# The FFN norm's sums and transposes at fixed early places, and groups of 4, 9 and 9 FFN steps in place of 5, 9 and 8

## The chip, the cores and the metric

The kernel runs on one core of one Trainium2 chip. Its time is the device time of one execution in microseconds (us). Five engines run their own queues of instructions and wait for each other by semaphores: TensorE (PE; its weight loads are PEld), VectorE (DVE), ScalarE (ACT), GpSimd (POOL) and SyncE (SP), which here issues the loads from memory.

## The reference

Two layers of a decoder trunk on a sequence of 512 with a model width of 1024: three mixers side by side, then a gated MLP. What the change touches is the MLP of each layer, all in float32:

```python
h = rmsnorm(x, norm_ffn_g[l])
gu = jnp.einsum('bsd,df->bsf', h, w_ffn_in[l])
g_ff, u_ff = gu[..., :D_FF], gu[..., D_FF:]
g_ff = causal_dwconv(g_ff, ffn_conv_w[l], ffn_conv_b[l])
x = x + jnp.einsum('bsf,fd->bsd', jax.nn.silu(g_ff) * u_ff, w_ffn_out[l])
```

`rmsnorm` divides x by the root of the mean of its squares over the 1024 channels and multiplies by a gain. D_FF is 2816 = 22 x 128.

## The kernel before

**Tiles.** x lies transposed in eight tiles x[0] to x[7] of 128 channels by 512 positions. A float32 product is made of three matmuls (`mm3`, L159 to L161): each operand is split into a high part, rounded to float32r on ACT (`hi_...`, L150 or L166), and the rest, computed on DVE (`lo_...`, L151 or L167), and PE adds hi x hi, hi x lo and lo x hi into one PSUM tile. The names of loads, casts and splits follow the tile: raw_w2, hi_w2, lo_w2.

**The FFN** (`ffn`, once per layer) has 22 steps of 128 channels of D_FF, in groups. For each group the steps make their activations act0, act1, ..., and then `rows` adds the group's share of the down projection to x, one output tile d after the other: its PSUM tiles are called p2, the group, d (p203 is group 0, d = 3). Group 0's steps are `plain`, the others `seven`.

- `plain(f)`: pg is the gate projection (8 x 3 matmuls of 512 columns on xg, the split x), pu the upper one (as many). DVE multiplies pg by the norm (rB, into pad), convolves it (c, with ACT's share), ACT applies SiLU, DVE forms u = pu x rB x c, and ACT and DVE split it into act.
- `seven(f)` makes both projections with seven products of half size (Strassen-Winograd): 7 x 4 x 3 matmuls of 256 columns into the PSUM tiles pa and pb. It needs sums of weight blocks (s31, s24, on DVE, split to h31, l31, h24, l24) and X[0] to X[3], sums of the *normalised* x.
- `halves(k)` makes X[k]: two tiles of x times gain and rB (xn), four sums of them (xt), and their splits. The list `todo` holds k = 0 to 3; a call is made after some steps of group 0 and the last one in its rows.
- The norm (`norm_x`): squares of x[k] on ACT, added on DVE (ssf), summed over channels by four small matmuls (pssf), the inverse root on DVE (twelve tiny instructions on rf), four transposes on PE (prf), and a copy on ACT to rB. In the FFN it is called in plain step 0, between pg and pu.

**Buffers that set the order.** Weights are loaded into a ring of four raw tiles (tag raw). Their splits have three slots when a load is more than 512 wide and two (tag "b") when it is 512 or less. `rows` loads a row's weights in one load of width x 128 columns, or in two (512 and the rest) when the group has more than eight steps: 640 for five steps, 512 and 640 for nine, 1024 for eight. PSUM has four tiles for projections.

**What sets the order.** The code is recorded instruction by instruction; a scheduler then orders each engine's instructions by its own model of time, by priority (weight loads and splits, and the blocks of seven steps that make weight sums, have high priority) and by what is free. Each engine runs its list in that order. `tc.keep_in_program_order` holds an instruction at its recorded place.

Of the kernel before, what the change touches and what calls it, by code (L numbers as in the profile page):

```python
# [15 lines left out]
ALU = mybir.AluOpType  # L16
# [4 lines left out]
P = 128  # L21
# [6 lines left out]
DFF = 2816  # L28
FT = DFF // P

GROUPS = (5, 9, 8)
HALF = S // 2
BUCKETS = 32
MAX_DIST = 128
# [19 lines left out]
def trunk(ctx, tc, xT, wr, wh, wt, wda, wret, wsc, wo, wf, w2, par, lamp, relb, onehot, mask, rope, gtab, out):  # L54
# [14 lines left out]
    def temp(name, w=S):  # L69
        return tp.tile([P, w], F32, tag="s", name=name, bufs=6, padded_shape=[P, S])  # L70
# [62 lines left out]
    def load_w(src, name):  # L133
        n = int(np.prod(src.shape[1:]))
        with tc.high_priority():
            raw = wp.tile([P, n], F32, tag="raw", bufs=4, name="raw_" + name, padded_shape=[P, D])
            ordered(nc.sync.dma_start(raw if len(src.shape) == 2 else raw.rearrange("p (b n) -> p b n", b=src.shape[1]), src))
        return raw

    def split_w(raw, name):  # L140
        n = int(np.prod(raw.shape[1:]))
        with tc.high_priority():
            tag, bufs = ("", HL) if 2 * n > D else ("b", 2)
            hi, lo = [
                wp.tile([P, n], F32R, tag=t + tag, name=f"{t}_{name}", padded_shape=[P, D if n > D // 2 else D // 2], bufs=bufs)
                for t in ("hi", "lo")
            ]
            flat = len(raw.shape) == 2
            h, w = [t if flat else t.rearrange("p (b n) -> p b n", b=raw.shape[1]) for t in (hi, lo)]
            A.copy(h, raw)  # L150
            V.tensor_tensor(w, raw, h.bitcast(F32), ALU.subtract)  # L151
        return hi, lo
# [90 lines left out]
    def norm_x(name):  # L243

        ss = temp(f"ss{name}")
        A.activation(ss, x[0], AF.Square)
        for k in range(1, KT):
            sq = temp(f"sq{k}{name}")
            A.activation(sq, x[k], AF.Square)
            V.tensor_tensor(ss, ss, sq, ALU.add)  # L250
        ps = aux(f"pss{name}")
        for st in range(ST):
            T.matmul(ps[:, st : st + 1], ss[:, st * P : (st + 1) * P], ones[:, 0:1], start=True, stop=True)
        ms = small(4, f"ms{name}")
        V.tensor_scalar(ms, ps[:, 0:4], 1.0 / D, EPS, ALU.mult, ALU.add)
        r = sp.tile([P, 4], F32, tag="r", name=f"r{name}", bufs=2)
        rsqrt(r, ms, 4, name)
        pr = transposes(lambda st: r[:, st : st + 1].broadcast_to([P, P]), f"pr{name}")
        rB = sp.tile([P, S], F32, tag="rB", name=f"rB{name}", bufs=1)
        A.copy(rB, pr)  # L260
        return r, rB

    def project(xg, ps, w):

        for k, xk in enumerate(xg):
            sl = slice(k * P, (k + 1) * P)
            mm3(ps, (w[0][:, sl], w[1][:, sl]), xk, k == 0, k == len(xg) - 1)

# [9 lines left out]
    def transposes(src, name):  # L278

        ps = aux(name)  # L280
        for st in range(ST):
            T.transpose(ps[:, st * P : (st + 1) * P], src(st), ident)
        return ps

    def conv(dst, padt, wcol, bcol):
# [458 lines left out]
    def ffn(l, fp):  # L744
# [3 lines left out]
        pt = pars[l]  # L748
        L = f"L{l}"
        xg = [split_x(l, G_FFN, f"f{L}", k) for k in range(KT)]  # L750
        norm = []
        X = [fp.tile([P, 2, 7, HALF], F32R, name=f"X{k}{L}") for k in range(KT // 2)]

        def sums4(name):
# [20 lines left out]
        def plain(f):  # L775
            both = wf[l, f].rearrange("p (b n) -> p b n", n=S)
            ps = main(f"pg{f}{L}")
            project(xg, ps, split_w(load_w(both[:, 1::2], f"fg{L}{f}"), f"fg{L}{f}"))
            if not norm:
                norm.append(norm_x(f"f{L}")[1])  # L780
            padt = pads[f % 2]
            V.tensor_tensor(padt[:, 2 : S + 2], ps, norm[0], ALU.mult)
            c = temp(f"c{f}{L}")
            wc = FF_W + 3 * f
            conv(c, padt, lambda t: pt[:, wc + t : wc + t + 1], pt[:, FF_B + f : FF_B + f + 1])
            A.activation(c, c, AF.Silu)
            ps = main(f"pu{f}{L}")
            project(xg, ps, split_w(load_w(both[:, 0::2], f"fu{L}{f}"), f"fu{L}{f}"))
            u = temp(f"u{f}{L}")
            V.tensor_tensor(u, ps, norm[0], ALU.mult)  # L790
            V.tensor_tensor(u, u, c, ALU.mult)
            return split2(u, pairN(f"act{f}{L}"))

# [184 lines left out]
```

## Time and profile before

| | us |
|---|---|
| runs: median, lowest, highest of 3 | 1524.24, 1523.73, 1524.32 |
| the profiled execution, its span | 1523.98, 1522.2 |
| granted TensorE clock, mean | 1.000 |
| FFN of layer 0: plain steps start, rows of group 0 start, first seven step starts | 413.35, 469.18, 497.87 |
| FFN of layer 1: the same | 1167.46, 1223.28, 1251.96 |

All places are us from the span's start. In a row of the timeline stand start, duration, engine, line, operation, output<-inputs, and in brackets how long the engine had been idle and what ended that. Durations overlap a little at the ends, so costs in a row of equal work are better read from start to start.

### The profile page before, as it was taken

What the parts mean: (1) busy time and instruction counts of PE and PEld (TensorE: products, weight loads), DVE (VectorE), ACT (ScalarE), POOL (GpSimd) and SP (SyncE); (2) the same over time, 40 slices, a digit from 0 to 9 for tenths busy, and PEclk for the clock granted to TensorE, in tenths of its full rate; (3) what the DMA queues carried; (4) which work ended last, traced back from release to release, by engine and by line L of the source; (5) the groups of instructions that cost most, each with busy time, mean ns of one, the idle gap of its engine ahead of it and who ended that gap; (6) DMA issues with size and microseconds to landing.
All of it is one profiled execution on the core that took longest, in us unless ns stands there. A gap on an engine that the chain in (4) does not pass through costs nothing.

```text
span 1522.2 us, 22065 instructions
## 1 busy us (share of the span) xinstructions
PE 1513.5 (99%) x8510; PEld 1339.4 (88%) x8510; DVE 1103.4 (72%) x2074; ACT 733.5 (48%) x1304; POOL 13.0 (1%) x26
## 2 busy tenths in 40 slices
PE   9999999999999999999999999999999999999998
PEld 7899988888887999899789999888888889988996
DVE  8588787554669996796656887865545899957963
ACT  4555665333445564464425565643333556634641
POOL 1000000000000000000100000000000000000000
PEclk9999999999999999999999999999999999999999
DMA  6322222232323322522422222222322233234322
GB/s 212 115 73 81 87 84 90 76 104 83 108 71 108 116 93 72 169 84 84 132 76 93 74 91 87 83 84 83 110 85 89 80 109 111 88 93 139 112 60 80
DMA packets 51145, 147.24 MB, mean 97 GB/s; under 512 B 5623, under 2 KB 6022, under 8 KB 51040
## 3 DMA queue, kind: packets, MB, share of 16 engines
q1 hardware_dynamic: 50224, 143.38, 28.5%
q0 software_dynamic: 816, 2.46, 0.6%
q8 instruction: 67, 1.10, 0.3%
q14 instruction: 38, 0.31, 0.1%
HBM read 143.70 MB, written 2.11 MB: 96 GB/s over the span
## 4 chain that ended last, share of the span: by engine, by line
PE 96%; DVE 2%; DMA 1%; issue 0%; ACT 0%; SPq 0%; ACTq 0%; DVEq 0%
PE pnrvgL L161 1%; PE pnrvgL L159 1%; PE pnrvgL L160 1%; PE pnrqkL L160 1%; PE pnrqkL L161 1%; PE pnrqkL L159 1%; PE pnh2L L161 1%; PE pnh2L L159 1%; PE pnh3L L160 1%; PE pnh3L L161 1%; PE pnh1L L161 1%; PE pnh2L L160 1%; PE pnh3L L159 1%; PE pnh1L L160 1%; PE pnh0L L159 1%; PE pnh1L L159 1%
## 5 line engine op out<-in xcount | busy, mean ns | idle before, releaser
L150 ACT CAST hi_tL<-raw_tL 128x1024 fp32r<-128x1024 f32 x60 | 62.9, 1049 | 115.6 <-issue 14.7
L150 ACT CAST hi_w2L<-raw_w2L 128x640 fp32r<-128x640 f32 (+2 forms) x64 | 49.5, 782 | 86.8 <-PE p214L L160 10.4
L151 DVE TENSOR_TENSOR lo_tL<-raw_tL,hi_tL 128x1024 fp32r<-128x1024 f32 x60 | 73.4, 1223 | 15.9 <-ACT hi_tL L150 15.6
L151 DVE TENSOR_TENSOR lo_w2L<-raw_w2L,hi_w2L 128x640 fp32r<-128x640 f32 (+2 forms) x64 | 56.0, 886 | 28.7 <-ACT hi_w2L L150 28.7
L150 ACT CAST hi_fbL<-raw_f1L 128x1024 fp32r<-128x1024 f32 x34 | 35.7, 1050 | 38.8 <-PE pa8L L160 6.8
L151 DVE TENSOR_TENSOR lo_fbL<-raw_f1L,hi_fbL 128x1024 fp32r<-128x1024 f32 x34 | 41.4, 1219 | 5.1 <-ACT hi_fbL L150 5.0
L150 ACT CAST hi_oL<-raw_oL 128x1024 fp32r<-128x1024 f32 x16 | 16.9, 1054 | 58.1 <-issue 25.2
L150 ACT CAST hi_faL<-raw_f0L 128x512 fp32r<-128x512 f32 x34 | 21.1, 622 | 28.1 <-DMA raw_f0L<-in_wf 10.0
L151 DVE TENSOR_TENSOR lo_fuL<-raw_fuL,hi_fuL 128x1024 fp32r<-128x1024 f32 x10 | 12.2, 1223 | 19.6 <-ACT hi_fuL L150 19.6
L151 DVE TENSOR_TENSOR lo_faL<-raw_f0L,hi_faL 128x512 fp32r<-128x512 f32 x34 | 23.3, 684 | 3.7 <-ACT hi_faL L150 3.7
L150 ACT CAST hi_fuL<-raw_fuL 128x1024 fp32r<-128x1024 f32 x10 | 10.5, 1051 | 31.1 <-issue 17.5
L150 ACT CAST hi_nrvgL<-raw_nrvgL 128x1024 fp32r<-128x1024 f32 x8 | 8.4, 1050 | 29.7 <-PE pnrvgL L161 13.5
L150 ACT CAST hi_fgL<-raw_fgL 128x1024 fp32r<-128x1024 f32 x10 | 10.5, 1054 | 24.1 <-issue 16.0
L151 DVE TENSOR_TENSOR lo_oL<-raw_oL,hi_oL 128x1024 fp32r<-128x1024 f32 x16 | 19.6, 1224 | 2.8 <-ACT hi_oL L150 2.8
L151 DVE TENSOR_TENSOR lo_nrvgL<-raw_nrvgL,hi_nrvgL 128x1024 fp32r<-128x1024 f32 x8 | 9.8, 1221 | 12.5 <-ACT hi_nrvgL L150 12.5
L151 DVE TENSOR_TENSOR lo_nh0L<-raw_nh0L,hi_nh0L 128x768 fp32r<-128x768 f32 x8 | 7.6, 956 | 13.1 <-ACT hi_nh0L L150 13.1
L150 ACT CAST hi_bdL<-raw_bdL 128x512 fp32r<-128x512 f32 x16 | 9.9, 618 | 12.6 <-issue 4.2
L150 ACT CAST hi_nrqkL<-raw_nrqkL 128x1024 fp32r<-128x1024 f32 (+1 forms) x9 | 8.4, 947 | 13.9 <-issue 13.9
L150 ACT CAST hi_nh0L<-raw_nh0L 128x768 fp32r<-128x768 f32 x8 | 6.7, 838 | 15.2 <-PE pnh0L L161 7.8
L151 DVE TENSOR_TENSOR lo_fgL<-raw_fgL,hi_fgL 128x1024 fp32r<-128x1024 f32 x10 | 12.2, 1221 | 2.2 <-ACT hi_fgL L150 2.2
L151 DVE TENSOR_TENSOR lo_nrqkL<-raw_nrqkL,hi_nrqkL 128x1024 fp32r<-128x1024 f32 (+1 forms) x9 | 9.8, 1103 | 5.2 <-ACT hi_nrqkL L150 5.2
L150 ACT CAST hi_nh3L<-raw_nh3L 128x768 fp32r<-128x768 f32 x8 | 6.7, 838 | 11.5 <-PE ptg16L L160 5.3
(8471 smaller groups left out, 5967.6 us busy)
## 6 DMA issues: line engine op xcount, KB each, us to landing
raw_tL<-in_wt SPq DMA_DIRECT2D x60, 512.0 KB, 3.3
raw_f0L<-in_wf SPq DMA_DIRECT2D x34, 512.0 KB, 3.7
raw_f1L<-in_wf SPq DMA_DIRECT2D x34, 512.0 KB, 3.7
raw_w2L<-in_w SPq DMA_DIRECT2D x32, 320.0 KB, 2.9
raw_oL<-in_wo SPq DMA_DIRECT2D x16, 512.0 KB, 3.4
raw_w2L<-in_w SPq DMA_DIRECT2D x16, 512.0 KB, 3.5
raw_fgL<-in_wf SPq DMA_DIRECT2D x10, 512.0 KB, 4.0
raw_fuL<-in_wf SPq DMA_DIRECT2D x10, 512.0 KB, 4.0
```

Source lines behind the costliest of these rows:

```text
L150: A.copy(h, raw)
L151: V.tensor_tensor(w, raw, h.bitcast(F32), ALU.subtract)
L159: T.matmul(o, a[0], b[0], start=start, stop=False, skip_group_check=more)
L160: T.matmul(o, a[0], b[1], start=False, stop=False, skip_group_check=more)
L161: T.matmul(o, a[1], b[0], start=False, stop=stop, skip_group_check=more)
```

## The change

The norm becomes a generator in two steps. Its first step (squares, additions, pssf) is taken inside the gate projection of plain step 0, ahead of k = 6, its second (root, transposes, rB) inside the upper projection, ahead of k = 5; both are recorded at high priority, the first matmul of each is held in program order, and the matmuls recorded after each are issued behind it (`issue_after`, until step 1 is recorded). For that, step 0 records both projections before its convolution, and every plain step splits its upper weights before it. The groups become 4, 9 and 9. `halves` is called after steps 1, 2 and 3 and after the first of the rows.

```diff
-GROUPS = (5, 9, 8)
+GROUPS = (4, 9, 9)
@@ in norm_x, now norm_steps
         for st in range(ST):
-            T.matmul(ps[:, st : st + 1], ss[:, st * P : (st + 1) * P], ones[:, 0:1], start=True, stop=True)
+            i = T.matmul(ps[:, st : st + 1], ss[:, st * P : (st + 1) * P], ones[:, 0:1], start=True, stop=True)
+            if not st:
+                begin(i)
+        yield i
...
-        return r, rB
+        yield r, rB
 
-    def project(xg, ps, w):
+    def project(xg, ps, w, at=None, between=None):
 
         for k, xk in enumerate(xg):
+            if k == at:
+                pinned[0] = True
+                late.enter_context(tc.issue_after(between().ins))
+                pinned[0] = False
             sl = slice(k * P, (k + 1) * P)
             mm3(ps, (w[0][:, sl], w[1][:, sl]), xk, k == 0, k == len(xg) - 1)
@@ in ffn
+        steps = norm_steps(f"f{L}")
         norm = []
+
+        def rooted():
+            with tc.high_priority():
+                norm.append(next(steps)[1])
+            return turned[0]
+
+        def summed():
+            with tc.high_priority():
+                return next(steps)
@@ in plain
-            project(xg, ps, split_w(load_w(both[:, 1::2], f"fg{L}{f}"), f"fg{L}{f}"))
-            if not norm:
-                norm.append(norm_x(f"f{L}")[1])
+            project(xg, ps, split_w(load_w(both[:, 1::2], f"fg{L}{f}"), f"fg{L}{f}"), *(() if f else (6, summed)))
+            pu = main(f"pu{f}{L}")
+            wu = split_w(load_w(both[:, 0::2], f"fu{L}{f}"), f"fu{L}{f}")
+            if not f:
+                project(xg, pu, wu, 5, rooted)
             padt = pads[f % 2]
...
-            ps = main(f"pu{f}{L}")
-            project(xg, ps, split_w(load_w(both[:, 0::2], f"fu{L}{f}"), f"fu{L}{f}"))
+            if f:
+                project(xg, pu, wu)
             u = temp(f"u{f}{L}")
-            V.tensor_tensor(u, ps, norm[0], ALU.mult)
+            V.tensor_tensor(u, pu, norm[0], ALU.mult)
@@ in the loop over the groups
                 act.append(seven(f) if grp else plain(f))
-                if grp == 0 and f >= 2 and len(todo) > 1:
+                if f == 1:
+                    late.close()
+                if grp == 0 and f and todo:
                     halves(todo.pop(0))
             for d in range(KT):
                 rows(grp, f0, act, d)
-                if todo and d == 1:
+                if todo:
                     halves(todo.pop(0))
```

`turned[0]` is the last transpose, set by `transposes`; `begin` holds its instruction in program order while `pinned[0]` is set. The lines of the file move by up to 38 (a DVE product at L790 stands at L826 after).

What this does to the engines' lists is shown at three places of layer 0. Rows read: line, operation, output<-inputs, the output's shape, and how many alike.

**The norm on PE.** Before, the four sums stood behind all of pg0 and a part of pu0:

```order
L161 MATMUL pg0L_3929<-xs7fL_3922,lo_fgL_3933 128x512
L160 MATMUL pu0L_4016<-xs3fL_3910,hi_fuL_4019 128x512
L253 MATMUL pssfL_3983<-ones,ssfL_3960 128x1 x4
L161 MATMUL pu0L_4016<-xs3fL_3910,lo_fuL_4020 128x512
L159 MATMUL pu0L_4016<-xs4fL_3913,hi_fuL_4019 128x512
```

Now they stand ahead of pg0's k = 6:

```order
L160 MATMUL pg0L_3929<-xs5fL_3916,hi_fgL_3932 128x512
L161 MATMUL pg0L_3929<-xs5fL_3916,lo_fgL_3933 128x512
L266 MATMUL pssfL_3977<-ones,ssfL_3954 128x1 x4
L159 MATMUL pg0L_3929<-xs6fL_3919,hi_fgL_3932 128x512
L160 MATMUL pg0L_3929<-xs6fL_3919,hi_fgL_3932 128x512
```

That is 17 matmuls earlier. The transposes (prf) stood behind the last matmul of pg1 and now stand ahead of pu0's k = 5, 33 matmuls earlier.

**The end of group 0's steps on PE and DVE.** Before, PE did twelve matmuls each of rows d = 0, 1 and 2 (act0 to act3), and only then what needs act4:

```order
L160 MATMUL p202L_4455<-act3L_4287,hi_w2L_4458 128x512
L161 MATMUL p202L_4455<-act3L_4287,lo_w2L_4459 128x512
L159 MATMUL p200L_4394<-act4L_4376,hi_w2L_4397 128x512
L159 MATMUL p201L_4417<-act4L_4376,hi_w2L_4420 128x512
L159 MATMUL p202L_4455<-act4L_4376,hi_w2L_4458 128x512
L160 MATMUL p200L_4394<-act4L_4376,hi_w2L_4397 128x512
```

Now nine matmuls each of rows d = 0 and 1 stand ahead of the last activation, act3:

```order
L161 MATMUL p201L_4355<-act2L_4213,lo_w2L_4359 128x512
L159 MATMUL p200L_4320<-act3L_4302,hi_w2L_4323 128x512
L159 MATMUL p201L_4355<-act3L_4302,hi_w2L_4358 128x512
L160 MATMUL p200L_4320<-act3L_4302,hi_w2L_4323 128x512
L161 MATMUL p200L_4320<-act3L_4302,lo_w2L_4324 128x512
L160 MATMUL p201L_4355<-act3L_4302,hi_w2L_4358 128x512
L161 MATMUL p201L_4355<-act3L_4302,lo_w2L_4359 128x512
L159 MATMUL p202L_4375<-act0L_4050,hi_w2L_4378 128x512
```

On DVE, before, between u4 (the product of pu4 and rB, a few rows up) and act4's low half:

```order
L762 SCALAR_TENSOR_TENSOR xn7L_4442<-x_89,par_110,rBfL_4008 128x512
L151 TENSOR_TENSOR lo_w2L_4459<-raw_w2L_4456,hi_w2L_4458 128x640
L791 TENSOR_TENSOR u4L_4373<-u4L_4373,c4L_4337 128x512
L766 TENSOR_TENSOR xt2L_4383<-xn2L_4379 128x256
L167 TENSOR_TENSOR X2L_3927<-xn2L_4379,X2L_3927 128x256
```

And now, from u3 on:

```order
L826 TENSOR_TENSOR u3L_4299<-pu3L_4262,rBfL_4030 128x512
L796 SCALAR_TENSOR_TENSOR xn2L_4305<-x_84,par_110,rBfL_4030 128x512
L796 SCALAR_TENSOR_TENSOR xn6L_4307<-x_88,par_110,rBfL_4030 128x512
L796 SCALAR_TENSOR_TENSOR xn3L_4340<-x_85,par_110,rBfL_4030 128x512
L796 SCALAR_TENSOR_TENSOR xn7L_4342<-x_89,par_110,rBfL_4030 128x512
L827 TENSOR_TENSOR u3L_4299<-u3L_4299,c3L_4270 128x512
L800 TENSOR_TENSOR xt2L_4309<-xn2L_4305 128x256
L167 TENSOR_TENSOR X2L_3927<-xn2L_4305,X2L_3927 128x256
```

The rows that follow, up to the low half of the last activation, are the same eight before and now (sums and splits of X2 and X3, then act). The split lo_w2 of row d = 2 has moved from here to a place behind act3.

**The rows behind it on DVE, and the start of group 1 on ACT.** Before, behind act4 and three more sums:

```order
L852 SCALAR_TENSOR_TENSOR x_82<-p200L_4394,x_82 128x512
L852 SCALAR_TENSOR_TENSOR x_83<-p201L_4417,x_83 128x512
L151 TENSOR_TENSOR lo_w2L_4482<-raw_w2L_4479,hi_w2L_4481 128x640
L852 SCALAR_TENSOR_TENSOR x_84<-p202L_4455,x_84 128x512
L167 TENSOR_TENSOR X2L_3927<-xt2L_4383,X2L_3927 128x1024
L151 TENSOR_TENSOR lo_w2L_4505<-raw_w2L_4502,hi_w2L_4504 128x640
L167 TENSOR_TENSOR X3L_3928<-xt3L_4444,X3L_3928 128x1024
```

Now, behind act3 and the same three sums (the first lo_w2 here is of row d = 2, the second of d = 3):

```order
L888 SCALAR_TENSOR_TENSOR x_82<-p200L_4320,x_82 128x512
L151 TENSOR_TENSOR lo_w2L_4379<-raw_w2L_4376,hi_w2L_4378 128x512
L888 SCALAR_TENSOR_TENSOR x_83<-p201L_4355,x_83 128x512
L167 TENSOR_TENSOR X2L_3927<-xt2L_4309,X2L_3927 128x1024
L167 TENSOR_TENSOR X3L_3928<-xt3L_4344,X3L_3928 128x1024
L151 TENSOR_TENSOR lo_w2L_4399<-raw_w2L_4396,hi_w2L_4398 128x512
```

In the first seven steps ACT now has the casts of later steps ahead of the copies that empty pa4 and pa5:

```order
L150 CAST hi_fbL_4773<-raw_f1L_4753 128x1024
L150 CAST hi_faL_4755<-raw_f0L_4751 128x512
L858 COPY pad_115<-pa4L_4521 128x256
L858 COPY pad_116<-pa5L_4649 128x256
L150 CAST hi_faL_4883<-raw_f0L_4879 128x512
L862 COPY pad_115<-pa4L_4521 128x256
```

The cast hi_fa in the fifth row is of step 7; before, the second copy of the first seven step's pa stood ahead of the cast of step 8, three steps on. In layer 1 the lists are the same, except that X2's cast and split stand ahead of row d = 2's.

More of the change, by code (lines that the diff above doesn't have):

```diff
@@ L243, in norm_x, with begin, norm_steps @@
     def norm_x(name):
+        *_, last = norm_steps(name)
+        return last
+    pinned, turned, late = [False], [None], ExitStack()
+    def begin(i):
+        if pinned[0]:
+            tc.keep_in_program_order(i)
+        return i
+    def norm_steps(name):
         ss = temp(f"ss{name}")
@@ L281, in transposes @@
         for st in range(ST):
-            T.transpose(ps[:, st * P : (st + 1) * P], src(st), ident)
+            i = T.transpose(ps[:, st * P : (st + 1) * P], src(st), ident)
+            if not st:
+                begin(i)
+        turned[0] = i
         return ps
```

## Prediction

> **What bounds the kernel now.** I read the page first, then who waits for whom on TensorE, then busy time by stage, and last the rows of the stage that the change touches.
>
> ```profile
> span 1522.2 us, 22065 instructions
> PE 1513.5 (99%) x8510; PEld 1339.4 (88%) x8510; DVE 1103.4 (72%) x2074; ACT 733.5 (48%) x1304; POOL 13.0 (1%) x26
> ```
>
> TensorE (PE) is busy in 1513.5 of 1522.2 us. So there are only two ways to gain: fewer matmul columns, or the few places where PE stands still. The view of PE's waits names the latter (total, times, longest):
>
> ```profile
> PE p204L L159 <- ACT hi_w2L L150: 1.6, 2, 0.8
> PE pa5L L159 <- ACT pad L822: 0.6, 1, 0.6
> PE p224L L159 <- ACT hi_w2L L150: 0.4, 2, 0.2
> PE p225L L159 <- ACT hi_w2L L150: 0.4, 2, 0.2
> ```
>
> All four are in the FFN: in the rows of group 0 (p20), at the first seven step (pa5, layer 1 alone), and in the rows of group 2 (p22). By stage (start:end, length, then busy time of PE, PEld, DVE, ACT, POOL, clock, DMA):
>
> ```profile
> 413.35:469.18 55.83, 55.83 (x254) 46.32 (x252) 41.71 (x70) 26.33 (x34) 0.00 (x0) 1.00 0.24 75
> 458.30:469.18 10.88, 10.88 (x50) 9.01 (x48) 10.31 (x18) 5.62 (x8) 0.00 (x0) 1.00 0.21 60
> 469.18:497.87 28.69, 27.80 (x121) 22.31 (x120) 27.74 (x45) 15.08 (x20) 0.00 (x0) 1.00 0.37 121
> 497.87:580.00 82.13, 82.13 (x686) 82.13 (x685) 77.26 (x109) 50.00 (x85) 0.00 (x0) 1.00 0.32 106
> 597.70:637.62 39.92, 39.92 (x179) 33.03 (x177) 27.55 (x38) 14.95 (x21) 0.00 (x0) 1.00 0.44 145
> 1223.28:1251.96 28.68, 27.80 (x122) 22.32 (x120) 27.07 (x44) 14.47 (x20) 0.00 (x0) 1.00 0.36 116
> 1251.96:1334.90 82.94, 82.34 (x686) 82.14 (x685) 77.89 (x109) 50.65 (x86) 0.00 (x0) 1.00 0.33 107
> ```
>
> These are, for layer 0, the five plain steps, the last of them alone, the rows of group 0, group 1's seven steps and most of its rows; then the two early stages again for layer 1. The third row matters most: in the rows of group 0 the **vector engine (DVE)** is busy in 27.74 of 28.69 us, as full as PE. Whatever makes this stage shorter for PE without taking as much from DVE opens a wait.
>
> **The work on PE.** A plain step is 48 matmuls of 512 columns in 10.88 us, 0.2267 each. A seven step has 7 x 4 x 3 = 84 of 256 columns; twelve take 1.44 us:
>
> ```profile
> 1253.39 0.28 PE L159 MATMUL pb5L<-X0L,h315L 128*128 128x256 f32 x1
> 1254.83 0.28 PE L159 MATMUL pa6L<-X0L,hi_faL 128*128 128x256 f32 x1
> ```
>
> So a seven step is 10.08 us. Per layer one step changes kind: -0.80 us, **-1.60** in all. The rows keep their 22 x 8 x 3 matmuls.
>
> **The norm.** The sums and transposes stay the same instructions on PE, 17 matmuls earlier for the sums and 33 for the transposes.
>
> ```profile
> 413.55 0.69 DVE L742 SCALAR_TENSOR_TENSOR x<-po7L,x 128x512 f32<-128x512 f32 x1 [2.05 <-PE po7L L161]
> 423.30 0.15 DVE L255 TENSOR_SCALAR msfL<-pssfL 128x4 f32<-128x4 f32 x1
> 425.47 0.16 DVE L237 SCALAR_TENSOR_TENSOR rfL<-ntfL,rfL 128x4 f32<-128x4 f32 x1
> ```
> ```profile
> 421.29 0.95 PE L253 MATMUL pssfL<-ones,ssfL 128*128 128x1 f32 x8
> 430.63 0.60 PE L282 MATMUL prfL<-ident,rfL 128*128 128x128 f32 x4
> ```
>
> The sums would now issue at 413.35 + 18 x 0.2267 = 417.4, the transposes near 423. The last square is added on DVE at about 416.3 (x7 is ready at 414.2, one weight split of 1.14 and one addition of 0.6 follow), and the root takes 2.3 us from about 418.4, so neither should hold PE. I cost the pin at nothing on PE; if the addition came late, every matmul behind the sums would wait with them, bounded by 1.5 us a layer. What it gives is 33 x 0.2267 = 7.5 us by which DVE can start on step 0 earlier. That covers DVE's work up to the last plain step's u and no further: u3 (and all that stands behind it on DVE) waits for the last matmul of pu3, whatever came before.
>
> **Rows of group 2.** With eight steps each load is 1024 wide and lies in three slots held until the last step arrives; then PE waits twice per layer:
>
> ```profile
> 735.15 0.39 PE L160 MATMUL p223L<-act14L,hi_w2L 128*128 128x512 f32 x1
> 735.76 0.50 PE L159 MATMUL p224L<-act14L,hi_w2L 128*128 128x512 f32 x1 [0.21 <-ACT hi_w2L L150]
> 736.09 0.40 PE L160 MATMUL p224L<-act14L,hi_w2L 128*128 128x512 f32 x1
> 736.70 0.51 PE L159 MATMUL p225L<-act14L,hi_w2L 128*128 128x512 f32 x1 [0.21 <-ACT hi_w2L L150]
> ```
>
> Start to start 0.61 in place of 0.23, twice: 0.76. Group 1, nine wide with loads of 512 and 640, shows none (39.92 of 39.92 above), and group 2 now has that form: **-1.52** for two layers. Between 0 and -1.52 I take the whole, by group 1's row.
>
> **Rows of group 0: the wait for the last plain step.** This is the term that decides. Before:
>
> ```profile
> 469.18 0.39 PE L159 MATMUL p200L<-act0L,hi_w2L 128*128 128x512 f32 x1
> 477.79 0.39 PE L159 MATMUL p202L<-act4L,hi_w2L 128*128 128x512 f32 x1
> 478.26 0.50 PE L160 MATMUL p200L<-act4L,hi_w2L 128*128 128x512 f32 x1
> 478.60 0.40 PE L161 MATMUL p200L<-act4L,lo_w2L 128*128 128x512 f32 x1
> ```
> ```profile
> 469.38 0.69 DVE L790 TENSOR_TENSOR u4L<-pu4L,rBfL 128x512 f32<-128x512 f32 x1 [0.73 <-PE pu4L L161]
> 472.64 0.81 DVE L151 TENSOR_TENSOR lo_w2L<-raw_w2L,hi_w2L 128x640 fp32r<-128x640 f32 x1
> 473.37 0.68 DVE L791 TENSOR_TENSOR u4L<-u4L,c4L 128x512 f32<-128x512 f32 x1
> 473.97 0.41 DVE L766 TENSOR_TENSOR xt2L<-xn2L 128x256 f32<-128x256 f32 x1
> 477.53 0.68 DVE L167 TENSOR_TENSOR act4L<-u4L,act4L 128x512 fp32r<-128x512 f32 x1
> ```
>
> Between u4 and the low half of act4 DVE also does most of halves(2) and halves(3): 8.15 us. PE had 39 matmuls of rows d = 0, 1, 2 to do meanwhile, 8.84 us, so it would have asked at 478.02 and started at 478.26: a loss of 0.24. Now the same rows stand between u3 and act3, less one weight split (0.73): 7.42 us. But PE has only 2 x 9 + 2 = 20 matmuls ahead, 4.53 us: the loads are 512 wide, that kind has two slots, so row d = 2 can't be loaded until row 0 is done. The plain stage ends 10.88 earlier, at 458.30; u3 starts at 458.50, act3's low half at 465.92, done 466.60, PE goes on at 466.65 in place of 462.83: **3.82 us lost** in each layer. This hangs on no estimate but that the durations stay.
>
> **The rows behind it.** Walking DVE's and ACT's new order on from 466.6, in layer 0, with these durations:
>
> ```profile
> 478.84 0.73 ACT L150 CAST hi_w2L<-raw_w2L 128x640 fp32r<-128x640 f32 x1 [4.13 <-PE p200L L160]
> 481.66 1.21 DVE L167 TENSOR_TENSOR X2L<-xt2L,X2L 128x1024 fp32r<-128x1024 f32 x1
> 482.80 0.81 DVE L151 TENSOR_TENSOR lo_w2L<-raw_w2L,hi_w2L 128x640 fp32r<-128x640 f32 x1
> 483.64 0.33 SPq L137 DMA_DIRECT2D raw_f0L<-in_wf  x1
> 487.42 0.62 ACT L150 CAST hi_faL<-raw_f0L 128x512 fp32r<-128x512 f32 x1 [1.99 <-DMA raw_f0L<-in_wf]
> ```
>
> Row 2's cast starts 0.58 after p200's last use (478.84 - 478.26), at 467.23, and ends 0.62 later; its low half on DVE follows three 256-column sums and an x (0.33 and 0.60 start to start) and ends at 468.81. PE, free at 467.68, gets two matmuls in and waits: 0.72. Then one x, X2 and X3 (1.14 each) stand ahead of row 3's low half, done at 472.28 where PE asks at 471.68: 0.65. In layer 1 X2's cast and split stand ahead of row 2's: about 0.9 more. Before, this part lost 1.49 in the stage, first wait included (28.69 - 120 x 0.2267).
>
> **The start of group 1.** A raw slot is reused in a ring of four: before, f0 of the first seven step left 0.03 after a row's split ended (483.61) and its first reader ran 3.78 later. Now the fifth row's split ends at 473.5, the eighth's near 485.5, and DVE makes f0's and f1's sums in between; the first split sum of step 4 (l31) comes out at 484.9, PE asks at 483.9: about 0.95. Then on ACT the copy that frees pa4 stands behind the cast of step 7's f0, which lands near 497.2 (issued at 493.4): the copy ends at 498.1, PE asks at 496.9: about 1.2. These two are the softest numbers. Bounds: 0 (everything lands earlier, as in layer 0 before, where group 1 has 82.13 of 82.13) and twice as much. I take the walk's value. After that DVE needs some 9.4 us for a seven step's 10.08 (77.26 of 82.13), so it catches up and group 1 goes on without waits.
>
> Each of five waits also costs 0.11 in the restart (478.26 to 478.60 in place of 0.23): 0.5.
>
> Layer 0: 3.82 + 0.72 + 0.65 + 0.95 + 1.2 + 0.5 = 7.84 for 1.49 before: +6.35. Layer 1: 8.74 for 1.48 + 0.81 before (28.68 - 27.2; 82.94 - 82.13): +6.45. **Sum:** 12.80 - 1.60 - 1.52 = +9.7 us on the profiled execution's 1523.98 (median of the runs 1524.24, lowest 1523.73): **1533.7 us**, 0.6% slower.
>
> **The rule on the clock.** The granted clock is 1.00 in every row above, the gaps of 0.8 to 1.0 us included; a gap of 3 us doesn't occur. The Trainium skill, "TensorE: Matmul & The Clock Gate", section "What's actually happening", says that the array falls to half its clock after an idle window of some 3.4 us. By that rule a wait of 3.1 us (the longer of the two pieces of the 3.82) would mostly just escape, and the sum would stay.
>
> **Rivals.**
> 1. *Only the first wait counts.* The rows and group 1 absorb the rest, as layer 0's group 1 did before. Per layer 3.82 + 0.72 + 0.65 + 0.3 restart = 5.5, so 11.0 - 3.8 - 3.1 = +4.1: 1528.1. For it: landings spread by a microsecond. Against: DVE is full here.
> 2. *The clock drops.* If PE ran at half speed for as long as it had stood (3.1 us), it would lose 1.55 more per layer, or the pinned sums would hold PE as much: +3.1, 1536.8. The page named above gives the half clock; no trace here shows one.
> 3. *Faster: the earlier norm takes halves(2) and halves(3) out of the wait.* It decides if they are done before pu3 ends. Then act3 is late by nothing and the p20 and pa5 waits go: -1.60 - 1.52 - 1.49 - 2.29 = -6.9: 1517.1. DVE would have the time (it idles 14 us in the five plain steps, 55.83 - 41.71), but in the new order all of halves(2) and (3) stand behind u3.
> 4. *The change does little*: the waits are half of what I count and the gains pay for the rest, 1525.
>
> **How the numbers follow.** Forecast 0.62 (1530.5 to 1536.5), rival 1 0.15, rival 2 0.12, rival 4 0.06, rival 3 0.05. The range 1528 to 1538 leaves out about 0.2: rivals 3 and 4, the low half of 1 and a little of 2. A measurement of this kernel tells some 0.2% (3 us) from no change: faster 0.05; within 0.2% rival 4 and the lowest part of rival 1, 0.08; slower 0.87.
>
> **What would show it.** PE's waits should have the first rows of act3 (p200, L160) waiting for DVE act3 for about 3 us in both layers, hi_w2 or lo_w2 waits at p202 and p203, a wait for the pad copy at the second seven product of step 4, and none at p224 and p225. A stage of group 0's rows longer than 21.76 us by 5 or more confirms the walk. If act3's low half starts within 5 us of u3, or the halves run before u3, I am wrong and the time falls. If the clock column shows less than 1.00 behind the wait, rival 2 holds.

## The result and the profile after

| | before | after |
|---|---|---|
| median of 6 runs, us | 1524.28 | 1533.58 |
| lowest, highest | 1523.73, 1524.96 | 1532.95, 1535.02 |
| profiled execution, its span | 1523.98, 1522.2 | 1533.46, 1531.7 |

The ratio is 1.0059 (95% interval 1.0049 to 1.0069): 9 us slower, where 1533.7 was predicted. The page's line of the engines (busy time, share, instructions) has TensorE busy 2.0 us longer, though it has fewer columns to do:

```profile
PE 1515.5 (99%) x8582; PEld 1344.0 (88%) x8582; DVE 1114.7 (73%) x2102; ACT 742.7 (48%) x1332; POOL 13.0 (1%) x26
```

The view of TensorE's waits (total, times, longest):

```profile
PE p200L L160 <- DVE act3L L167: 5.5, 2, 2.8
...
PE p200L L159 <- ACT act3L L166: 1.2, 2, 0.6
...
PE pb4L L161 <- DVE l314L L167: 1.1, 2, 0.7
PE p202L L159 <- ACT hi_w2L L150: 1.1, 1, 1.1
```

The four waits of before (p204, pa5, p224, p225) are gone, and one new wait, for act3, is larger than all of them. It is the one the prediction was built on. DVE's timeline from u3 to act3's low half:

```profile
458.63 0.69 DVE L826 TENSOR_TENSOR u3L<-pu3L,rBfL 128x512 f32<-128x512 f32 x1 [1.42 <-PE pu3L L161]
...
466.03 0.69 DVE L167 TENSOR_TENSOR act3L<-u3L,act3L 128x512 fp32r<-128x512 f32 x1
```

466.03 - 458.63 = 7.40, where 7.42 was forecast. DVE is idle for 1.42 just ahead of u3: the early norm had let it catch up, and then it had to wait for pu3 all the same. TensorE's timeline at this place and behind it:

```profile
462.28 0.39 PE L161 MATMUL p201L<-act2L,lo_w2L 128*128 128x512 f32 x1
463.28 0.50 PE L159 MATMUL p200L<-act3L,hi_w2L 128*128 128x512 f32 x1 [0.60 <-ACT act3L L166]
463.61 0.40 PE L159 MATMUL p201L<-act3L,hi_w2L 128*128 128x512 f32 x1
466.78 0.50 PE L160 MATMUL p200L<-act3L,hi_w2L 128*128 128x512 f32 x1 [2.77 <-DVE act3L L167]
...
467.99 0.50 PE L159 MATMUL p202L<-act0L,hi_w2L 128*128 128x512 f32 x1
...
468.99 0.79 PE L161 MATMUL p202L<-act0L,lo_w2L 128*128 128x512 f32 x1
469.58 0.63 PE L159 MATMUL p202L<-act1L,hi_w2L 128*128 128x512 f32 x1
470.00 0.63 PE L160 MATMUL p202L<-act1L,hi_w2L 128*128 128x512 f32 x1
```

From start to start, less the 0.227 of a matmul, TensorE loses 0.77 and 2.94 here: 3.71. The last two rows show what the forecast left out of its sum: matmuls that follow each other at 0.43 instead of 0.227. The windows view says why (start:end, length, busy time of PE, PEld, DVE, ACT, POOL, then the granted clock, DMA share, GB/s); the stretches are 3.41 us long, laid out from where the clock column changes:

```profile
461.60:465.01 3.41, 1.80 (x7) 0.86 (x5) 3.41 (x9) 1.37 (x3) 0.00 (x0) 1.00 0.00 0
465.01:468.42 3.41, 1.63 (x6) 0.97 (x6) 3.41 (x9) 1.10 (x2) 0.00 (x0) 1.00 0.00 0
468.42:471.83 3.41, 3.28 (x9) 2.27 (x8) 3.41 (x5) 1.94 (x3) 0.00 (x0) 0.50 0.27 77
471.83:475.24 3.41, 3.41 (x17) 2.77 (x16) 1.86 (x3) 0.62 (x1) 0.00 (x0) 1.00 0.29 82
1222.77:1226.18 3.41, 1.20 (x4) 0.67 (x4) 3.34 (x8) 0.97 (x2) 0.00 (x0) 1.00 0.00 0
1226.18:1229.59 3.41, 2.52 (x5) 1.60 (x6) 3.30 (x4) 2.07 (x4) 0.00 (x0) 0.50 0.00 0
1229.59:1233.00 3.41, 3.41 (x9) 2.64 (x9) 0.86 (x2) 0.00 (x0) 0.00 (x0) 0.50 0.54 154
```

After the stall the granted clock is half of full for one such stretch in layer 0 and for two in layer 1.

**The ledger.** Each term is what TensorE's matmuls took from start to start beyond 0.227 (512 columns) or 0.120 (256), in us per layer:

| | forecast L0, L1 | measured L0, L1 |
|---|---|---|
| a plain step becomes a seven step | -0.80, -0.80 | -0.80, -0.80 (by column counts) |
| waits in the rows of group 2 | -0.76, -0.76 | -1.27, -1.27 |
| wait for act3 | 3.82, 3.82 | 3.93, 3.93 |
| rows 2 and 3 behind it | 1.37, 2.27 | 2.17, 4.58 |
| start of group 1 | 2.15, 2.15 | 1.05, 1.58 |
| restarts | 0.50, 0.50 | in the three rows above |
| waits of before in group 0's rows and at pa5 | -1.49, -2.29 | -1.44, -2.30 |
| sum | 4.8, 4.9 | 3.64, 5.72 |

The measured sums are 9.36; 0.1 more stands outside the two FFNs, together the 9.48 between the profiled executions.

### The profile page after: what moved, and what is told of

It reads as the page before. It is cut to its first block, busy times and chain, and to the rows that moved or that the text cites. A ratio compares the mean times of both kernels' runs of the same rounds, so it can differ in the third digit from the quotient of the medians.

```text
span 1531.7 us, 22316 instructions
## 1 busy us (share of the span) xinstructions
PE 1515.5 (99%) x8582; PEld 1344.0 (88%) x8582; DVE 1114.7 (73%) x2102; ACT 742.7 (48%) x1332; POOL 13.0 (1%) x26
## 4 chain that ended last, share of the span: by engine, by line
PE 95%; DVE 3%; DMA 1%; issue 0%; ACT 0%; SPq 0%; DVEq 0%; ACTq 0%
PE pnrvgL L161 1%; PE pnrvgL L159 1%; PE pnrvgL L160 1%; PE pnrqkL L160 1%; PE pnrqkL L161 1%; PE pnrqkL L159 1%; PE pnh2L L161 1%; PE pnh2L L159 1%; PE pnh3L L160 1%; PE pnh3L L161 1%; PE pnh1L L161 1%; PE pnh2L L160 1%; PE pnh3L L159 1%; PE pnh1L L160 1%; PE pnh1L L159 1%; PE pnh0L L160 1%
## 5 line engine op out<-in xcount | busy, mean ns | idle before, releaser
L150 ACT CAST hi_w2L<-raw_w2L 128x512 fp32r<-128x512 f32 (+1 forms) x80 | 52.8, 665 | 107.2 <-PE p222L L160 10.6
L151 DVE TENSOR_TENSOR lo_w2L<-raw_w2L,hi_w2L 128x512 fp32r<-128x512 f32 (+1 forms) x80 | 58.9, 742 | 46.4 <-ACT hi_w2L L150 46.3
L150 ACT CAST hi_nh2L<-raw_nh2L 128x768 fp32r<-128x768 f32 x8 | 6.7, 840 | 10.4 <-PE ptsc21L L160 9.2
```

## The experiments

Each run has a name, e1 to e12 (in its diff, ... stands for lines that are left out); the figures behind its heading are the ratio of its time to the kernel before's and its 95% interval. The kernel before ran beside each of them and took 1525.4 to 1525.8 us there (median), 1.1 to 1.5 more than above, so ratios to before are what is compared; the changed kernel's is 1.0059. Waits and losses are in us from start to start, as in the ledger.

**e1: the norm pinned, nothing else** (the changed kernel edited; 1.0001, 0.9993 to 1.0010)

```diff
-GROUPS = (4, 9, 9)
+GROUPS = (5, 9, 8)
...
-                if grp == 0 and f and todo:
+                if grp == 0 and f >= 2 and len(todo) > 1:
...
-                if todo:
+                if todo and d == 1:
```

> The norm tied to its early places, but the groups 5, 9, 8 and the halves where they were before. Theory (the pin costs nothing on TensorE, and what it gives DVE reaches no further than the last plain step's u): within 0.5 us of before, 1523.5 to 1524.8, the waits of p204 on hi_w2, of p224 and p225 and layer 1's pa5 all still there, and the first row of act4 late by 0.2 to 0.3 as before. Rival 1 (the pinned sums hold TensorE until the squares are added): +1 to +3 us, 1525 to 1527, with a wait of pss on DVE in each layer. Rival 2 (the earlier norm empties DVE's queue through the rows of group 0): the p204 wait of 0.8 goes in both layers, -1.5 to -3 us.

The theory holds. The pinned sums and transposes cost TensorE 0.10 and 0.09 a layer, exactly what the scheduler's places cost before, and the 0.24 and 0.96 at act4 and p204 are still there. One place differs: TensorE waits for the pad copy at pa5 in both layers (0.84 and 1.20), where the kernel before had 0.75 in layer 1 alone. But e3, whose edit does not touch that place, has 1.06 and 1.04 there, so a difference of that size at pa5 can't be put down to an edit.

**e2: the groups and the halves' places, no pin** (the kernel before edited; 1.0071, 1.0057 to 1.0085)

```diff
-GROUPS = (5, 9, 8)
+GROUPS = (4, 9, 9)
...
-                if grp == 0 and f >= 2 and len(todo) > 1:
+                if grp == 0 and f and todo:
...
-                if todo and d == 1:
+                if todo:
```

> Groups 4, 9, 9 and the halves in their new places, the norm left to the scheduler as before. Theory (the stall comes from the groups alone; u3 waits for pu3 whatever the norm did): 1533.5 within 1.5 us, p200 waits 2.8 to 3.0 for act3's low half in both layers. Rival (the pin pays here): in the profile of the changed kernel DVE stands idle 6.2 us in all between the first use of the norm and u3, and without the pin the norm comes 7.5 us later, so u3 would start 1 to 1.5 us late and the wait for act3 grow to 4 to 4.5 us in each layer: 1536 to 1538.

Between the two, and the interval touches the changed kernel's. The stall is there without the pin: it comes from the groups. The first wait for act3 is 1.20 in place of 0.77, so without the pin u3 is 0.4 late, not 1 to 1.5. In the profiled execution the half clock lasts three stretches of 3.41 in both layers, as the windows view of e2 shows in its clock column:

```profile
465.51:475.75 10.24, 8.28 (x18) 5.58 (x19) 7.23 (x12) 3.03 (x4) 0.00 (x0) 0.50 0.19 51
1226.69:1236.93 10.24, 8.20 (x18) 5.50 (x19) 7.32 (x13) 3.03 (x4) 0.00 (x0) 0.50 0.17 51
```

The mean clock of that execution is 0.993. Of the other four one has 0.993 too, and three have 0.996, as the changed kernel has in five of its six. So the longer half clock can't be put down to the missing pin.

**e3: rows of eight steps in two loads** (the kernel before edited; 0.9990, 0.9981 to 0.9999)

```diff
-            edge = min(width, KT // 2) if width > KT else 0
+            edge = min(width, KT // 2) if width >= KT else 0
```

> The kernel before with one edit: the rows of the group with eight steps load their weights in two halves of 512 columns as the rows with nine steps do. Theory (the waits in the rows of group 2 come from the 1024 wide loads alone): the p224 and p225 waits and their restarts go, 1.27 us in each layer, so 1524.3 - 2.5 = 1521.7; with the size that the prediction gave the term (0.76 a layer) 1522.7. Rival (the waits come from ACT's or DVE's order at the end of group 2, not from the width): they stay, 1524.0 to 1524.6.

The waits at p223 to p225 (1.27 a layer) go, and one of 0.42 + 0.11 comes at p221: 0.74 a layer gained, 1.5 in all instead of 2.5, which the ratio agrees with. So the width of the load is the cause, and nine steps in the group are worth 0.5 a layer more than eight with the same two loads.

**e4: matmuls that nobody reads, in the stall** (the changed kernel edited, in `mm3` and `rows`; 1.0038, 1.0026 to 1.0051)

```diff
+FEED = 12
...
-        T.matmul(o, a[1], b[0], start=False, stop=stop, skip_group_check=more)
+        return T.matmul(o, a[1], b[0], start=False, stop=stop, skip_group_check=more)
...
+                        if grp == 0 and n == 3 and d == 1:
+                            o = aux(f"idle{L}")
+                            with tc.issue_after(last.ins), tc.high_priority():
+                                for i in range(FEED):
+                                    T.matmul(o, w[0][:, :P], act[2][0], start=True, stop=True)
-                        mm3(ps, (w[0][:, sl], w[1][:, sl]), act[n], n == 0, n == width - 1)
+                        last = mm3(ps, (w[0][:, sl], w[1][:, sl]), act[n], n == 0, n == width - 1)
```

> The changed kernel with 12 matmuls of 128x512 (2.7 us) whose result nobody reads, put between the third step's last matmul of row 1 and the first of act3, where TensorE stands. Theory (the half clock behind the wait comes from TensorE's standing there, and costs 0.2 us for every 512 column matmul that it meets): TensorE stands no longer than 1.2 us in one piece, the clock column shows 1.00 throughout, act3's low half comes at the same time, and the kernel is faster by 1.0 in layer 0 and 1.8 to 2.5 in layer 1: 1530 to 1531 with more work. Rival 1 (the slower matmuls have another cause than the standing, or the half clock costs nothing because the weights come late there anyway): 1533.5 within 0.5. Rival 2 (the added matmuls hold the others up): 1534.5 or more.

The theory holds: with 24 matmuls more, the kernel is some 3 us faster than the changed one (1.0038 against 1.0059). TensorE's timeline has it stand for 1.10 at act3:

```profile
463.31 2.88 PE L892 MATMUL idleL<-act2L,hi_w2L 128*128 128x512 f32 x12
466.03 0.39 PE L160 MATMUL p200L<-act3L,hi_w2L 128*128 128x512 f32 x1
466.25 0.39 PE L160 MATMUL p201L<-act3L,hi_w2L 128*128 128x512 f32 x1
467.58 0.50 PE L161 MATMUL p200L<-act3L,hi_w2L 128*128 128x512 f32 x1 [0.94 <-DVE act3L L168]
```

and the windows view of e4 has the clock whole behind it, as it is in layer 1:

```profile
463.20:475.00 11.80, 10.13 (x43) 7.42 (x42) 11.29 (x22) 4.49 (x7) 0.00 (x0) 1.00 0.15 44
```

The gain is not spread as expected. From the first matmul of plain step 0 to the last of p227, layer 1 is 353.31 long in place of 356.06, layer 0 353.04 in place of 353.23: there the wait for l314 grew from 0.61 to 1.27 and took back most of what the rows behind act3 gained. In layer 1 the gain is not the clock's alone: with the added matmuls the scheduler also ordered ACT otherwise. In the changed kernel the cast of X2 stands ahead of row 2's (ACT's timeline, layer 1):

```profile
1225.21 1.05 ACT L166 CAST X2L<-xt2L 128x1024 fp32r<-128x1024 f32 x1 [4.21 <-DVE xt2L L803]
1226.16 0.61 ACT L150 CAST hi_w2L<-raw_w2L 128x512 fp32r<-128x512 f32 x1
```

and in e4 behind it:

```profile
1225.71 0.62 ACT L151 CAST hi_w2L<-raw_w2L 128x512 fp32r<-128x512 f32 x1 [4.09 <-PE p200L L161]
1226.23 1.05 ACT L167 CAST X2L<-xt2L 128x1024 fp32r<-128x1024 f32 x1
```

TensorE's wait at p202 there is 0.17 in place of 1.24. So e4 shows that the stall brings the half clock; how much of the 3 us is the clock's and how much the order's it does not part.

**e5: the halves behind act3 on DVE** (the changed kernel edited, in `split` and in the loop over the groups; `lows[0]` is act3's low half; 1.0047, 1.0034 to 1.0059)

```diff
+    lows = [None]
...
-            V.tensor_tensor(lo, src, hi.bitcast(F32), ALU.subtract)
+            lows[0] = V.tensor_tensor(lo, src, hi.bitcast(F32), ALU.subtract)
...
-                if grp == 0 and f and todo:
+                if grp == 0 and f in (1, 2):
                     halves(todo.pop(0))
+            if not grp:
+                after3 = lows[0]
+                with tc.issue_after(after3.ins):
+                    halves(todo.pop(0))
             for d in range(KT):
                 rows(grp, f0, act, d)
                 if todo:
-                    halves(todo.pop(0))
+                    with tc.issue_after(after3.ins):
+                        halves(todo.pop(0))
```

> The changed kernel with DVE's part of halves(2) and halves(3) queued behind act3's low half; no work is added or left out. Theory (act3 is late because the halves stand ahead of it on DVE): u3, its product and the low half follow each other, the latter done near 461.5 where TensorE asks at 462.8; the p200 waits (3.93 with restarts, per layer) and the half clock (some 1.3 and 2.9) go. Against that DVE still has 22 us of work from u3 to l314 for 21.8 us of rows, so 1 to 2 us come back at the start of group 1 in each layer: 1521 within 1.5 us. Rival (DVE's work in the stage is the bound, the order on it does not matter): all of the 3.9 comes back as later waits (lo_w2, l314) and only the clock's part is saved, 1529 to 1531.

The theory fell: the ratio is only 0.12% below the changed kernel's, and the two intervals overlap. The rival's later waits came, and one stretch of half clock in each layer, which the rival had counted as saved. act3 is there in time, but the weights' low halves (lo_w2) now stand behind the halves on DVE, as TensorE's waits show:

```profile
PE p202L L161 <- DVE lo_w2L L151: 4.6, 2, 2.3
PE p204L L161 <- DVE lo_w2L L151: 2.1, 2, 1.4
PE p207L L161 <- DVE lo_w2L L151: 1.6, 1, 1.6
```

Here the same work put behind act3 only makes other rows late.

**e6: all four halves one step earlier** (the changed kernel edited; 1.0014, 1.0005 to 1.0023)

```diff
-                if grp == 0 and f and todo:
+                if grp == 0 and todo:
```

> The changed kernel with each of the four halves one step earlier: halves(0) behind plain step 0 (the pinned norm allows it), halves(3) behind plain step 3. Theory: DVE is idle 9.5 us of the 45 us of plain steps, so halves(0) to (2) are done before pu3 ends, and only halves(3) stands between u3 and act3: 3.8 us in place of 7.4, where TensorE has 4.5 us of rows ahead. No wait for act3, no half clock, no wait for l314; what is left are some 0.5 to 0.9 of waits for the weights of row 2, which has only two slots: 1518.5 within 1.5 us, faster than before. Rival 1 (the plain steps of group 0 can't take DVE's extra work without holding TensorE): waits in p1 and p2, 1522 to 1526. Rival 2 (the pin has to carry norm and halves and DVE falls behind by the lost 7.5 us again): u3 starts late, 1530 or more.

Better by 0.45%, not by the 1% expected. Four waits are left in both layers: 1.13 for act3 (its low half starts 4.47 after u3, not 3.8, and u3 itself 0.25 later than in the changed kernel), 0.91 and 0.82 for row 2's weights, and 1.27 for l314; layer 0 has one more of 0.59 for the weights of p207, layer 1 one of 0.42 for the pad copy. The wait for l314 is not for want of DVE's time; DVE's timeline has it wait for the loads of group 1:

```profile
475.90 0.69 DVE L836 TENSOR_TENSOR s314L<-raw_f0L 128x512 f32<-128x512 f32 x1 [1.54 <-DMA raw_f0L<-in_wf]
...
479.05 0.69 DVE L837 TENSOR_TENSOR s314L<-raw_f0L,raw_f1L 128x512 f32<-128x512 f32 x1 [1.26 <-DMA raw_f1L<-in_wf]
```

**e7: rows 2, 3 and 4 of group 0 in the slots of wide loads** (the changed kernel edited; `wider` is handed on to the split; 0.9972, 0.9962 to 0.9983; 1520.99 us)

```diff
-            tag, bufs = ("", HL) if 2 * n > D else ("b", 2)
+            tag, bufs = ("", HL) if 2 * n > D or wider else ("b", 2)
...
-                    w = weights(w2[l, d, :, (f0 + a) * P : (f0 + b) * P], f"w2{L}{grp}{d}{a}")
+                    w = weights(w2[l, d, :, (f0 + a) * P : (f0 + b) * P], f"w2{L}{grp}{d}{a}", grp == 0 and d in (2, 3, 4))
```

> The changed kernel with the weights of rows 2, 3 and 4 of group 0 put into the three slots of the wide loads, which the plain steps have done with, in place of the two narrow ones. DVE's order stays but for one more weight split (0.6) ahead of act3. Theory (the wait is act3's lateness less the rows that can be loaded): TensorE now has some 39 matmuls, 8.8 us, ahead of act3's low half, which is done 8.5 to 9 us after pu3: the wait falls from 3.71 to 0 to 0.4, row 2's waits and the half clock go, l314 stays at 0.6 to 1.3: 1520 within 1.5 us. Rival (the slots are not free in time, or the four raw buffers hold the loads up): waits for hi_w2 at p202 to p204 of 1 us or more in each layer, 1524 to 1530.

The theory holds: act3's low half is as late as ever, and TensorE has so much else to do that it doesn't notice. DVE's timeline of e7:

```profile
466.41 0.68 DVE L167 TENSOR_TENSOR act3L<-u3L,act3L 128x512 fp32r<-128x512 f32 x1
```

and TensorE's at the same place, with four rows done as far as they go without that half:

```profile
467.04 0.39 PE L159 MATMUL p203L<-act3L,hi_w2L 128*128 128x512 f32 x1
467.26 0.40 PE L160 MATMUL p200L<-act3L,hi_w2L 128*128 128x512 f32 x1
```

So the version with this edit is faster than both kernels. A wait of 1.74 (layer 0) and 0.85 (layer 1) is left in the first seven step, for a copy on ACT that is queued behind two casts, the first of which waits for a load (ACT's timeline of e7):

```profile
482.88 1.05 ACT L150 CAST hi_fbL<-raw_f1L 128x1024 fp32r<-128x1024 f32 x1 [1.46 <-DMA raw_f1L<-in_wf]
483.83 1.04 ACT L166 CAST h244L<-s244L 128x1024 fp32r<-128x1024 f32 x1
484.78 0.36 ACT L860 COPY u4L<-pb4L 128x256 f32<-128x256 f32 x1
```

**e8: the edits of e6 and e7 together** (0.9970, 0.9959 to 0.9980)

> Both edits of the two runs before this one together. Theory: nothing is late in group 0's rows; the time is the column count and what was left of waits outside: before's 1524.3 less 1.6 (one step changed per layer), 2.5 (rows of group 2), 2.9 (first waits of the rows) and 0.9 (layer 1's pa5), 1516.4, plus up to 1.5 where DVE is full at the start of group 1. Rival (one of the two suffices, the second adds nothing or takes DVE time from group 1): within 0.7 us of the better of the two.

The rival holds: nothing more than the slots alone. Waits of 0.7 for act3 and 0.85 for a cast at pa4 stand where the copy's wait stood.

**e9: only row 2 in a wide slot** (e7 edited; 1.0004, 0.9995 to 1.0014)

```diff
-                    w = weights(w2[l, d, :, (f0 + a) * P : (f0 + b) * P], f"w2{L}{grp}{d}{a}", grp == 0 and d in (2, 3, 4))
+                    w = weights(w2[l, d, :, (f0 + a) * P : (f0 + b) * P], f"w2{L}{grp}{d}{a}", grp == 0 and d == 2)
```

> The changed kernel with only row 2 of group 0 in a wide slot: one more row of cover. Theory (the wait is act3's lateness less the rows that TensorE can do without it, nine matmuls, 2.04 us, to a row): TensorE asks at pu3's end + 6.8 us, act3's low half is done 8.3 us after it as in the changed kernel, so the p200 wait for the low half is 1.5 us instead of 3.7 in both layers; one wait of that length does not bring the half clock. With the waits for the next weights (about 1 us a layer) staying and l314 a little longer: 1525 to 1526 where the kernel before is at 1524.3, a ratio of 1.0005 within 0.001. Rival 1 (one more row is as good as three): the ratio of e7, 0.997. Rival 2 (cover does not matter, the five rows of e7 helped in another way): 1.005.

The theory holds in size. The wait is 1.55 from start to start in both layers, and the clock stays whole. TensorE's timeline of e9:

```profile
464.51 0.39 PE L159 MATMUL p202L<-act3L,hi_w2L 128*128 128x512 f32 x1
466.29 0.50 PE L160 MATMUL p200L<-act3L,hi_w2L 128*128 128x512 f32 x1 [1.39 <-DVE act3L L167]
```

One row of cover takes 2.2 off the wait; three take all of it. Left are 0.73 for weights at p204 and some 2 in the first seven step of each layer, where the wait for l314 has gone and others, for casts and the pad copy, have come.

**e10: the pin and the halves' places with the groups of before** (the changed kernel edited; 0.9982, 0.9973 to 0.9991)

```diff
-GROUPS = (4, 9, 9)
+GROUPS = (5, 9, 8)
```

> The third part of the change without the groups: groups 5, 9, 8, the norm tied early, the halves in their new places (so halves(2) is behind plain step 3 and only halves(3) behind step 4). Theory: with five plain steps the halves gain a step, DVE's work between u4 and act4 falls from 8.1 to some 4.5 us, act4's low half is there before TensorE asks for it, the 0.24 wait at p200 goes, and p204's 0.98, which stands behind it, goes or shrinks: -0.5 to -2.9 us, ratio 0.998 to 0.9997. Rival (p204 waits because of the slots of the weights, whatever act4 does): p204's wait stays and the ratio is 1.000 within 0.0007.

The theory holds: faster than before. With five steps halves(2) lies behind step 3, act4's low half starts 474.52 - 469.31 = 5.2 after u4 instead of 8.15 (DVE's timeline of e10):

```profile
469.31 0.69 DVE L826 TENSOR_TENSOR u4L<-pu4L,rBfL 128x512 f32<-128x512 f32 x1 [0.73 <-PE pu4L L161]
...
474.52 0.68 DVE L167 TENSOR_TENSOR act4L<-u4L,act4L 128x512 fp32r<-128x512 f32 x1
```

and TensorE has no wait at p200 and p204 but some 0.3 of restarts (its timeline):

```profile
477.95 0.39 PE L160 MATMUL p200L<-act4L,hi_w2L 128*128 128x512 f32 x1
...
479.54 0.39 PE L160 MATMUL p203L<-act0L,hi_w2L 128*128 128x512 f32 x1
479.83 0.50 PE L159 MATMUL p204L<-act0L,hi_w2L 128*128 128x512 f32 x1
```

**e11: the wide slots without the pin** (e2 with the edit of e7; 0.9987, 0.9978 to 0.9996)

> The kernel of e7 (groups 4, 9, 9, halves in their new places, rows 2 to 4 of group 0 in wide slots) without the pin. Theory (the pin gives at most what e2 lost against the changed kernel, 0.4 us of act3's lateness a layer and the windows of half clock that it brought; with 40 matmuls of cover neither matters): within 1 us of e7, ratio 0.9965 to 0.9985. Rival (the pin is what makes the stage fit): a wait for act3 of 1 us or more in each layer, ratio 0.9990 or more.

Neither range holds the ratio; the rival's wait is there (1.31 for act3 in layer 0, 1.29 in layer 1). The split of X1's sums (1.22 on DVE), done before u3 with the pin, now stands between u3 and act3. So with the wide slots the pin takes this wait away; in time that is some 0.15%, at the edge of what the two intervals, which overlap, can tell.

**e12: everything but the regrouping** (e10 edited; 0.9975, 0.9965 to 0.9984; 1521.72 us)

```diff
-            edge = min(width, KT // 2) if width > KT else 0
+            edge = min(width, KT // 2) if width >= KT else 0
```

> The groups of before (5, 9, 8), the norm tied early, the halves one step earlier, and the eight wide rows loaded in two halves (e10 and e3 together): everything but the regrouping. Theory (the two gains lie in different stages and add up): 0.9982 x 0.9990, a ratio of 0.9972 within 0.0008, so as fast as e7 with its groups 4, 9, 9 and three slots, and the regrouping's 1.6 us of matmul columns is lost again in what it costs at the start of group 1. Rival (the later stage takes up what the earlier one gains, waits for landing weights): 0.9980 to 0.9990.

The theory holds: the gains of the two edits add up, and the groups 5, 9, 8 come out as fast as 4, 9, 9 with three more slots. The groups 5, 9, 8 with those slots were not run, so what the regrouping is worth when both have them stays open. The largest waits of TensorE that are left stand where group 1 or a layer begins:

```profile
PE pa5L L159 <- ACT pad L858: 2.3, 2, 1.6
PE pnrqkL L159 <- ACT hi_nrqkL L150: 1.5, 2, 0.9
```

## Why the prediction was right, and where it was not

1. **The wait that decides** was right in place, mechanism and size: 3.71 for 3.82. Four runs show the mechanism: without the pin the wait stays (e2), with DVE's order turned it moves to other rows (e5), and with more rows loaded ahead it shrinks by about the rows' own length (e9: 1.55 with one more, e7: none with three more).
2. **"That covers DVE's work up to the last plain step's u and no further"** holds for this kernel (the idle 1.42 ahead of u3). As a statement about the pin it was too narrow: with five plain steps the pin and the halves' new places together gain 0.18% (e10), and the pin alone nothing (e1). No run has five plain steps and the new places without the pin, so how much of that is the pin's is not shown. What the change took away with the fifth step was the place where that gain would have shown.
3. **The rows of group 2** were under-sized: 0.76 a layer for 1.27 measured. The step that failed is "start to start 0.61 in place of 0.23, twice"; each of these waits is followed by a restart of 0.11, and a third one stands at p223 (0.17 + 0.11).
4. **"By that rule ... the sum would stay"** failed, and with it the weight given to the half clock (rival 2, at 0.12). Both layers fell to half clock, the prediction's own sign for rival 2; with e4's matmuls in the stall neither did, so the stall was the cause. Counted in the changed kernel's rows, matmuls that follow each other at 0.43 in place of 0.227 cost some 1.3 in layer 0 and 2.6 in layer 1; rival 2 put 1.55 on each. All of the rows behind act3 lost 2.17 and 4.58 (in e4, with ACT in another order as well, 1.30 and 1.29). The wait of 0.65 that was forecast for row 3 did not show in layer 0, where the slower matmuls reached that row later.
5. **The start of group 1** was over-sized, by the pad copy: 1.2 forecast, nothing in layer 0 and 0.2 in layer 1 measured. In layer 0 the load landed 0.7 earlier than walked, and pa4 did not wait. ACT's timeline of the changed kernel:

```profile
496.49 0.62 ACT L150 CAST hi_faL<-raw_f0L 128x512 fp32r<-128x512 f32 x1 [1.07 <-DMA raw_f0L<-in_wf]
497.02 0.37 ACT L862 COPY pad<-pa4L 128x256 f32<-128x256 f32 x1
```

   Such a wait exists (the copy in e7); in e7 the waits ahead of it are gone. l314, forecast at 0.95, cost 0.61 and 0.84, and 0.44 more went into a short wait for the cast hi_fa ahead of it and two restarts.

So the total (+9.5 for +9.7) came out partly by luck, because errors cancelled. Over both layers the rows of group 2 (-1.0), the start of group 1 (-1.7) and the restarts counted apart (-1.0) stand against the rows behind act3 (+3.1), which hold the half clock's 3.9 that the sum left out. The main wait was right in mechanism and size; the half clock stood only in a rival, and that the total came so near is no merit of the sum.

## What to carry to other kernels

A step less in a stage also takes away the work under which the last step's latency was hidden; ask how many matmuls TensorE can do without the last activation, and count the weight slots, since here they were what limited it. Putting DVE's work behind the late activation moved the wait to other rows, while one more row in a wide slot removed 2.2 us of it and three removed it all. A stall can cost twice: once by itself and once by the half clock behind it, so a kernel that must stand may keep its clock with useless matmuls in the gap.

## What the runs showed of the clock

In the changed kernel no wait of TensorE is longer than 2.94 us, and up to its last matmul no stretch of 3.41 us is without matmuls. Yet the clock fell. Laying out 3.41 us stretches from the places where the clock column changes, TensorE's busy time in a stretch at full clock, and what followed (from the windows view of each kernel):

| kernel | stretch | PE busy | next stretch |
|---|---|---|---|
| changed | 465.01, 1222.77 | 1.63, 1.20 | half |
| changed | 461.60, 1219.35 | 1.80, 1.83 | full |
| e2 | 462.10, 1223.27 | 1.12, 1.18 | half |
| e2 | 1530.48 | 1.61 | full |
| e5 | 464.15, 1232.14 | 1.00, 1.67 | half |
| e5 | 1225.32 | 1.68 | full |
| e6 | 462.74 | 1.85 | full |
| e4 | 466.89 | 1.98 | full |

In these twelve stretches the border is at about half of a stretch, but it is not sharp in this measure: 1.67 us in e5 and 1.63 in the changed kernel were followed by half clock, 1.61 at the end of e2 by full clock (its windows view; the second row is the rest of the kernel, without a matmul):

```profile
1530.48:1533.89 3.41, 1.61 (x8) 0.99 (x6) 0.69 (x1) 0.00 (x0) 0.00 (x0) 1.00 0.06 23
1533.89:1536.05 2.16, 0.00 (x0) 0.00 (x0) 0.00 (x0) 0.00 (x0) 0.00 (x0) 1.00 0.23 85
```

The ends of matmuls are modelled in the profile, and nothing here shows what exactly is counted. To get the clock back took more than to keep it: a stretch at half clock with 2.52 us of matmuls (changed kernel, layer 1) and one with 2.97 (e2) were followed by another at half clock, one with 3.28 (layer 0) by full clock. The stretches keep their phase: in the changed kernel the two falls are 1226.18 - 468.42 = 757.76 apart, 222.0 times 3.413 (a third of e2's 10.24), and in e2 and e5 223.0 and 225.0 times. e5 shows what the phase does. TensorE stands 2.5 us at p202 in both layers; in layer 0 that fell into one stretch and brought the half clock, in layer 1 it was cut in two and did not. The windows view of e5, layer 0 and then the two stretches of layer 1:

```profile
464.15:467.56 3.41, 1.00 (x5) 0.31 (x3) 3.41 (x8) 0.82 (x2) 0.00 (x0) 1.00 0.00 0
1221.90:1225.32 3.42, 2.71 (x10) 1.30 (x8) 3.42 (x9) 2.50 (x5) 0.00 (x0) 1.00 0.00 0
1225.32:1228.73 3.41, 1.68 (x7) 1.42 (x8) 3.41 (x8) 0.00 (x0) 0.00 (x0) 1.00 0.19 42
```

The Trainium skill, "TensorE: Matmul & The Clock Gate", section "What's actually happening", gives a free-running window of 3413 ns, with which these distances agree, and puts the fall after an idle window of about 3.4 us. The trace does not agree with the latter: windows with up to 1.67 us of matmuls in them were followed by the half clock, and the measurement decides. A 512 column matmul at half clock followed the last one at 0.43 us in place of 0.227.
